# A norm's factor is moved from the hidden activations to the layer's outputs

## The chip, the cores and the metric

The kernel runs on one core of a Trainium2 chip. The metric is the device time of one execution in microseconds (us), the median of several runs. The core has five engines with queues of their own, each worked through in order: PE (TensorE, matmuls into PSUM), DVE (VectorE), ACT (ScalarE), POOL (GpSimd) and SP, which here only starts transfers. ACT starts some transfers too.

## The reference

One layer of a decoder on 1032 tokens (1024 of a prompt and 8 of a decode batch). Three head groups come first; the change lies behind them, in the output projection, the second norm and the feed-forward part:

```python
x = x + mix @ w_out                       # (1032, 1024)
h2 = rms_norm(x, norm2_g)                 # x * rsqrt(mean(x*x) + 1e-6) * g, per token
x = x + square(relu(h2 @ w_ff1)) @ w_ff2  # 1024 -> 4096 -> 1024
```

The factor of the norm is one positive number per token. Relu lets it through, the square squares it, and the second product is linear in it, so `1 / (mean(x*x) + 1e-6)` may multiply the squared activations or the 1024 outputs of the second product.

## The kernel before

Everything is kept with features on the 128 partitions and tokens along the columns. A tile of 1032 columns is cut in two halves of 516 (`TH`), and a half in two quarters of 258 (`TQ2`). The matmuls work on numbers that are split into a rounded part (hi) and a rest (lo): a `split` is a cast on ACT and a subtraction on DVE or POOL, and each product is three matmuls (hi·hi, hi·lo, lo·hi). In the profile a split of weights has the tile name `w`, one of activations `xy`, `xe`, `xf`, `xa` (first product) or `hf` (second).

`out_proj` makes x after the head groups in eight tiles, adds up their squares in the tile `r2` (shown as `r`), and at its end turns the sum into the factor: three matmuls with a tile of ones, and on DVE three scalings and three reciprocals of 344 columns each. `x_late` then makes the last forms of x that the first product needs.

Both feed-forward products use a scheme with seven block products in place of eight. The **first product** (`ffn_up`) runs over 16 items `j`. Each has seven products of 24 matmuls (168 in all), called 0 to 6 below. DVE adds the results out of PSUM (`t<-pq`), ACT applies relu and square to two tiles of 1032 columns, DVE multiplies each by `r2` (`t<-t,r`), makes four differences, and ACT's queue stores seven half tiles in DRAM (`hs`). PSUM has four buffers `pq`. The weights of an item come as four raw tiles (a11, a12, a21, a22), of which `w_forms` makes four sums s1 to s4 on POOL and seven splits; five of the splits are on POOL, two on DVE. Three more raw tiles per item go through `w_sums`, which makes sums for the second product (two on POOL). The seven raw tiles per item share six buffers (`wf` 2, `wf2` 4) in turn, so each load has to wait until the tile six places before it was read for the last time. The splits of weights have seven buffers (`w` 4, `w2` 3).

The **second product** (`ffn_down`) has seven groups in the order i = 5, 1, 6, 2, 7, 3, 4, each with four items o of 96 matmuls. Written (7,2) below is item o = 2 of group 7. In one item, the weights of the next are split (`w_tile`: four splits on POOL, in groups 7 and 3 each behind a subtraction of two raw tiles on DVE), the activations of the next group are loaded back and split on DVE (`hf`, two of 1032 columns per item, up to group 3), and the results are gathered in `p5`, `p1`, `u2` (shown as `acc`; `u3` is `u2`'s place, `u4` is `p1`'s). x itself comes back from DRAM by `x1` and is added on POOL, and `put` stores a half tile of the output from SP's queue. Results, loaded x and differences of weights share the six buffers `st` (`hx`).

The order on each queue is not the program's: a scheduler lays out all instructions before the run, by its own simulation, and the queues keep that order.

## Time and profile before

| | |
|---|---|
| median of 3 runs | 1522.04 us (1516.54 to 1531.46) |
| profiled execution | 1524.57 us, its span 1522.0 us |
| PE busy | 1384.9 us (91%) |
| DVE busy | 962.7 us (63%) |
| POOL busy | 824.2 us (54%) |
| ACT busy | 562.1 us (37%) |
| the first product on PE | 828.27 to 1185.31 us of the span |
| the second product on PE | 1185.31 us to the end |

The profile is one execution; all later stretches are microseconds from its start. PE is the busiest engine, but an average over 1522 us hides stages with different limits, so the stages have to be read one by one.

### The profile page before, as it was taken

The page shows a single profiled execution, that of the slowest core. Times are in us where ns is not written, and L with a number is a line of the kernel's source. Part 1 is how long each engine was busy: PE and PEld are TensorE (multiplying, and loading weights), DVE is VectorE, ACT ScalarE, POOL GpSimd, SP SyncE. Part 2 cuts the span into 40 slices and gives each one's busy share as a digit, 9 for nine tenths or more (in the row PEclk, how much of TensorE's full clock was granted, in tenths as well). Part 3 has the DMA queues.
Part 4 walks back from the last instruction along what each step waited for, and adds up shares of the span by engine and source line. Part 5 has one row for each costly group of instructions (what it writes and reads, how often), then busy time and mean ns, then how long its engine had stood idle before and what let it go on. Part 6 is the DMA issues. An engine that isn't in the chain of part 4 may idle for free.

```text
span 1522.0 us, 29392 instructions
## 1 busy us (share of the span) xinstructions
PE 1384.9 (91%) x11391; PEld 1276.8 (84%) x11391; DVE 962.7 (63%) x1656; ACT 562.1 (37%) x1057; POOL 824.2 (54%) x953
## 2 busy tenths in 40 slices
PE   5899799989889599797999699999999999999998
PEld 5888788879777477564898699999999999999998
DVE  7657457657666746775445987878778553328730
ACT  6433223233233243343444443444334454423430
POOL 7012673461144556350135887878778565678852
PEclk9899999899888667768899899999999999999999
DMA  6143233314433722234722265546655996469850
GB/s 236 61 162 111 86 89 101 94 58 122 118 114 95 187 66 54 79 100 128 287 84 98 76 216 202 194 172 212 215 209 195 356 319 199 148 220 306 286 171 35
DMA packets 152070, 238.17 MB, mean 156 GB/s; under 512 B 40851, under 2 KB 63340, under 8 KB 151788
## 3 DMA queue, kind: packets, MB, share of 16 engines
q1 hardware_dynamic: 132892, 191.77, 39.1%
q10 hardware_dynamic: 13824, 37.98, 6.4%
q0 software_dynamic: 5216, 6.56, 1.9%
q8 instruction: 89, 1.46, 0.4%
q14 instruction: 49, 0.40, 0.1%
HBM read 165.22 MB, written 72.08 MB: 156 GB/s over the span
## 4 chain that ended last, share of the span: by engine, by line
PE 43%; POOL 18%; DVE 12%; DMA 12%; issue 9%; ACT 3%; SPq 2%; POOLq 0%; DVEq 0%; ACTq 0%
PE pq L85 15%; PE d L85 14%; PE g L85 9%; POOL st L53 7%; POOL w L53 6%; POOL inv L53 5%; DMA wf<-in_w_ff 3%; PE cx L85 2%; DVE st L53 2%; SPq L82 2%; PE cy L85 2%; DMA qs<-xs 1%; PE g L89 1%; DMA x<-in_xT 1%; DVE F L53 1%
## 5 line engine op out<-in xcount | busy, mean ns | idle before, releaser
L85 PE MATMUL pq<-hf,w 128*128 128x258 f32 x2688 | 326.6, 284 | 6.1 <-ACT hf L76 2.8
L85 PEld LDWEIGHTS pq<-hf,w 128*128 128x128 f32 x2688 | 325.2, 190 | 7.4 <-ACT hf L76 3.0
L53 POOL TENSOR_TENSOR w<-wf,w 128x512 fp32r<-128x512 f32 x114 | 177.1, 1562 | 118.5 <-ACT w L76 118.4
L85 PE MATMUL d<-hbig,w 128*128 128x344 f32 (+2 forms) x1296 | 221.9, 327 | 19.3 <-ACT w L76 9.2
L85 PEld LDWEIGHTS d<-hbig,w 128*128 128x128 f32 x1296 | 202.3, 199 | 32.5 <-ACT w L76 10.4
L76 ACT CAST w<-wf 128x512 fp32r<-128x512 f32 x190 | 116.8, 618 | 217.2 <-PE pq L85 87.8
L53 POOL TENSOR_TENSOR w<-st,w 128x512 fp32r<-128x512 f32 x80 | 134.0, 1695 | 7.3 <-ACT w L76 7.3
L53 DVE TENSOR_TENSOR hf<-t,hf 128x1032 fp32r<-128x1032 f32 x56 | 97.2, 1776 | 54.6 <-ACT hf L76 54.6
L76 ACT CAST w<-st 128x512 fp32r<-128x512 f32 x96 | 58.9, 617 | 181.7 <-POOL st L53 78.6
L85 PE MATMUL pq<-xe,w 128*128 128x258 f32 x768 | 100.4, 291 | 10.6 <-POOL w L53 10.6
L85 PEld LDWEIGHTS pq<-xe,w 128*128 128x128 f32 x768 | 97.7, 197 | 11.6 <-POOL w L53 11.6
L53 DVE TENSOR_TENSOR t<-pq,t 128x516 f32<-128x516 f32 x112 | 75.9, 690 | 43.0 <-PE pq L85 41.0
L53 POOL TENSOR_TENSOR inv<-inv,blk 128x54 f32<-128x54 f32 (+24 forms) x217 | 71.3, 328 | 55.9 <-DMA out_state_p<-sl 20.3
L85 PE MATMUL pq<-xy,w 128*128 128x258 f32 x768 | 97.1, 286 | 1.6 <-DVE t L53 0.9
L85 PEld LDWEIGHTS pq<-xy,w 128*128 128x128 f32 x768 | 95.4, 193 | 2.7 <-ACT xy L76 1.7
L53 POOL TENSOR_TENSOR st<-wf,wf 128x512 f32<-128x512 f32 x48 | 69.9, 1455 | 40.0 <-DMA wf<-in_w_ff 27.7
L53 DVE TENSOR_TENSOR w<-wf,w 128x512 fp32r<-128x512 f32 x76 | 69.8, 919 | 29.2 <-ACT w L76 28.5
L53 POOL TENSOR_TENSOR inv<-inv,inv 128x54 f32<-128x54 f32 (+24 forms) x217 | 78.6, 362 | 15.9
L85 PE MATMUL pq<-xf,w 128*128 128x258 f32 x576 | 75.8, 288 | 11.6 <-DVE xf L53 8.3
L85 PEld LDWEIGHTS pq<-xf,w 128*128 128x128 f32 x576 | 72.8, 195 | 12.5 <-DVE xf L53 8.7
L53 DVE TENSOR_TENSOR t<-t,r 128x1032 f32<-128x1032 f32 x32 | 59.9, 1871 | 22.1 <-ACT t L73 22.0
L73 ACT ACTIVATE t<-t 128x1032 f32<-128x1032 f32 x64 | 68.1, 1064 | 14.5 <-DVE t L53 14.2
(405 smaller groups left out, 2620.1 us busy)
## 6 DMA issues: line engine op xcount, KB each, us to landing
wf<-in_w_ff SPq DMA_DIRECT2D x208, 256.0 KB
t<-hs SPq DMA_DIRECT2D x56, 516.0 KB
hs<-t ACTq DMA_DIRECT2D x48, 516.0 KB
wf<-in_w_in SPq DMA_DIRECT2D x34, 256.0 KB
tmp<-xs SPq DMA_DIRECT2D x32, 256.0 KB
wf<-s2s SPq DMA_DIRECT2D x32, 256.0 KB
x<-in_xT SPq DMA_DIRECT2D x8, 516.0 KB
xs<-xs SPq DMA_DIRECT2D x24, 172.0 KB
```

Of the source, the lines that this page charges most:

```text
L53: return (e or self.nc.vector).tensor_tensor(out, a, b, op=op)
L73: return self.nc.scalar.activation(out, a, f, **k)
L76: return self.nc.scalar.copy(out, a)
L82: return self.nc.sync.dma_start(out=out, in_=a)
L85: return self.nc.tensor.matmul(out, l, r, start=start, stop=stop, **k)
L89: return self.nc.tensor.transpose(out, a, ident)
```

## The change

The factor is no longer made at the end of `out_proj`. A new function `norm2` makes it after the eighth item of the first product, in two halves of 516 columns, with two of the PSUM buffers `pq`. The two multiplications per item of the squared activations are dropped. In the second product each output half tile is multiplied by the factor before x is added: twelve on DVE in `fin`, four on POOL (`u3`), four on DVE straight out of PSUM in the last group. The additions of x move behind the multiplications. Beside that, one split of weights per item of the first product, that of s3, goes from POOL to DVE.

```diff
@@ out_proj
-        for t0, tn in TG:
-            p = self.ps("g")
-            self.mm(p[:, :tn], self.ones, acc[:, t0:t0 + tn])
-            self.ts(acc[:, t0:t0 + tn], p[:, :tn], 1.0 / 1024, ALU.mult, 1e-6, ALU.add)
-            nc.vector.reciprocal(acc[:, t0:t0 + tn], acc[:, t0:t0 + tn])
@@ w_forms
         self.sub(s3, a11, a21, g)
-        r.append(self.w_form(s3, g))
+        r.append(self.w_form(s3, v))
@@
+    def norm2(self):
+        acc = self.r2
+        for h in range(2):
+            p = self.psp.tile([128, 2, 512], F32, name=self.nm("pq"), tag="pq", bufs=4)
+            for g in range(2):
+                self.mm(p[:, g, :TQ2], self.ones, acc[:, h * TH + g * TQ2:h * TH + g * TQ2 + TQ2])
+            sl = slice(h * TH, h * TH + TH)
+            self.ts(self.two(acc[:, sl]), p[:, :, :TQ2], 1.0 / 1024, ALU.mult, 1e-6, ALU.add)
+            self.nc.vector.reciprocal(acc[:, sl], acc[:, sl])
@@ ffn_up
                 self.act(h, h, AF.Relu)
                 self.act(h, h, AF.Square)
-                self.mul(h, h, self.r2)
@@
             up(j, ws)
             ws = nxt
+            if j == 7:
+                self.norm2()
@@ ffn_down
+            r2 = lambda t: self.r2[:, t * TH:t * TH + TH]
+
+            def fin(d, t, y):
+                self.mul(y, y, r2(t))
+                self.add(y, y, x1(d, t), g)
+                put(d, t, y)
@@
             elif i == 6:
                 plus(u2[:, o], p1[:, o])
-                self.add(p1[:, o], p1[:, o], x1(o, 0), g)
             elif i == 2:
                 y = self.hx()
                 plus(y, p1[:, o])
-                put(o, 0, y)
+                fin(o, 0, y)
                 self.add(u4[:, o], u2[:, o], p5[:, o], g)
-                self.add(p5[:, o], p5[:, o], x1(o + 4, 1), g)
-                self.add(u4[:, o], u4[:, o], x1(o, 1), g)
             elif i == 7:
                 plus(u3[:, o], u2[:, o])
                 y = self.hx()
                 self.add(y, u3[:, o], p5[:, o], g)
-                put(o + 4, 1, y)
+                fin(o + 4, 1, y)
+                self.mul(u3[:, o], u3[:, o], r2(0), g)
                 self.add(u3[:, o], u3[:, o], x1(o + 4, 0), g)
             elif i == 3:
                 y = self.hx()
                 plus(y, u4[:, o])
-                put(o, 1, y)
+                fin(o, 1, y)
             else:
                 y = self.hx()
-                plus(y, u3[:, o])
+                self.mul(two(y), p, two(r2(0)))
+                self.add(y, y, u3[:, o])
                 put(o + 4, 0, y)
```

Three places in the laid-out order follow. In these rows the numbers behind a name tell tiles apart.

**First place: POOL between two items of the first product, before.** `st` with two `wf` inputs or `st` and `wf` is a sum, `w` a split. The third row is s4, which reads raw tile a12 (`wf_9515`) for the last time; the row `w_9771` splits the next item's a11 (`wf_9763`), which is loaded into the same buffer.

```order
666 L53 TENSOR_TENSOR st_9537<-wf_1366_9513,wf_1368_9517 128x512
667 L53 TENSOR_TENSOR w_1375_9534<-st_9527,w_1375_9534 128x512
668 L53 TENSOR_TENSOR st_9542<-wf_9515,st_9528 128x512
669 L53 TENSOR_TENSOR w_9531<-st_9528,w_9531 128x512
670 L53 TENSOR_TENSOR w_1377_9539<-st_9537,w_1377_9539 128x512
671 L53 TENSOR_TENSOR w_9771<-wf_9763,w_9771 128x512
672 L53 TENSOR_TENSOR st_9757<-wf_1393_9753,wf_1394_9755 128x512
673 L53 TENSOR_TENSOR w_9774<-wf_1398_9765,w_9774 128x512
674 L53 TENSOR_TENSOR st_9758<-st_9757,wf_9751 128x512
675 L53 TENSOR_TENSOR st_9777<-wf_1399_9767,wf_9769 128x512
```

The same place on POOL after:

```order
662 L53 TENSOR_TENSOR st_9519<-wf_1363_9495,wf_1365_9499 128x512
663 L53 TENSOR_TENSOR w_1372_9516<-st_9509,w_1372_9516 128x512
664 L53 TENSOR_TENSOR st_9524<-wf_9497,st_9510 128x512
665 L53 TENSOR_TENSOR w_9513<-st_9510,w_9513 128x512
666 L53 TENSOR_TENSOR w_9751<-wf_9743,w_9751 128x512
667 L53 TENSOR_TENSOR st_9737<-wf_1390_9733,wf_1391_9735 128x512
668 L53 TENSOR_TENSOR w_9754<-wf_1395_9745,w_9754 128x512
669 L53 TENSOR_TENSOR st_9738<-st_9737,wf_9731 128x512
670 L53 TENSOR_TENSOR st_9757<-wf_1396_9747,wf_9749 128x512
```

The split of s3 (`w_1377_9539<-st_9537`) is gone, so one instruction instead of two stands between s4 and the split of the next a11.

**Second place: DVE at the end of the eighth item of the first product, before.** The tiles of this item are `t_1505` to `t_1507`; the first two rows are its last two results out of PSUM, `t_1537` is the next item's first.

```order
1332 L53 TENSOR_TENSOR t_1506_10551<-pq_10684,t_1506_10551 128x516
1333 L53 TENSOR_TENSOR t_1507_10552<-pq_10714,t_1507_10552 128x516
1334 L53 TENSOR_TENSOR t_1506_10551<-t_1506_10551,r_7742 128x1032
1335 L53 TENSOR_TENSOR w_10547<-wf_10519,w_10547 128x512
1336 L53 TENSOR_TENSOR t_1505_10550<-t_1506_10551 128x516
1337 L53 TENSOR_TENSOR w_1503_10544<-st_10542,w_1503_10544 128x512
1338 L53 TENSOR_TENSOR t_1507_10552<-t_1507_10552,r_7742 128x1032
1339 L53 TENSOR_TENSOR t_1537_10801<-pq_10829,t_1536_10800 128x516
1340 L53 TENSOR_TENSOR t_1505_10550<-t_1507_10552,t_1505_10550 128x516
```

The same place on DVE after; here the eighth item's tiles are `t_1502` to `t_1504`, and `t_1536` is the next item's:

```order
1320 L53 TENSOR_TENSOR t_1503_10525<-pq_10658,t_1503_10525 128x516
1321 L53 TENSOR_TENSOR w_1498_10513<-st_10511,w_1498_10513 128x512
1322 L53 TENSOR_TENSOR t_1504_10526<-pq_10687,t_1504_10526 128x516
1323 L53 TENSOR_TENSOR t_1502_10524<-t_1503_10525 128x516
1324 L67 TENSOR_SCALAR r_7742<-pq_10723 128x516
1325 L53 TENSOR_TENSOR w_10521<-wf_10493,w_10521 128x512
1326 L67 TENSOR_SCALAR r_7742<-pq_10728 128x516
1327 L53 TENSOR_TENSOR w_1500_10518<-st_10516,w_1500_10518 128x512
1328 L1364 RECIPROCAL r_7742<-r_7742 128x516 x2
1329 L53 TENSOR_TENSOR t_1502_10524<-t_1504_10526,t_1502_10524 128x516
1330 L53 TENSOR_TENSOR t_1503_10525<-t_1504_10526,t_1503_10525 128x516
1331 L53 TENSOR_TENSOR t_1536_10783<-pq_10811,t_1535_10782 128x516
```

The two multiplications by `r` are gone in every item; the split of s3 (`w_1498`) has come in, and in this one item the scalings and the two reciprocals stand ahead of the next item's first result.

**Third place: POOL during items (7,0) and (7,1) of the second product, before.** The first row is the output sum of (7,0), `st_15183` that of (7,1); `acc` with `st` is an addition of x, `w` a split of weights.

```order
881 L53 TENSOR_TENSOR st_15033<-acc_12740,acc_12738 128x516
882 L53 TENSOR_TENSOR w_14922<-st_14920,w_14922 128x512
883 L53 TENSOR_TENSOR w_15045<-st_15043,w_15045 128x512
884 L53 TENSOR_TENSOR w_2035_15054<-st_15052,w_2035_15054 128x512
885 L53 TENSOR_TENSOR acc_12740<-acc_12740,st_15036 128x516
886 L53 TENSOR_TENSOR w_2039_15063<-st_15061,w_2039_15063 128x512
887 L53 TENSOR_TENSOR st_15183<-acc_12740,acc_12738 128x516
```

The same place on POOL after, where the two output sums are `st_14979` and `st_15134`:

```order
857 L53 TENSOR_TENSOR st_14979<-acc_12706,acc_12704 128x516
858 L53 TENSOR_TENSOR w_14868<-st_14866,w_14868 128x512
859 L53 TENSOR_TENSOR acc_12706<-acc_12706,r_7742 128x516
860 L53 TENSOR_TENSOR w_14996<-st_14994,w_14996 128x512
861 L53 TENSOR_TENSOR w_2027_15005<-st_15003,w_2027_15005 128x512
862 L53 TENSOR_TENSOR st_14979<-st_14979,st_14982 128x516
863 L53 TENSOR_TENSOR acc_12706<-acc_12706,st_14987 128x516
864 L53 TENSOR_TENSOR w_2031_15014<-st_15012,w_2031_15014 128x512
865 L53 TENSOR_TENSOR st_15134<-acc_12706,acc_12704 128x516
```

From one output sum to the next there are eight instructions instead of six; the two new ones are the multiplication of u3 by `r` and the addition of x to the output, which waits for a multiplication on DVE.

## Rows read from the trace of the kernel before

**Rows 1.** Windows by stage: start:end, length, then per engine busy us (count), clock, DMA
```profile
822.00:828.27 6.27, 3.23 (x9) 1.34 (x8) 5.80 (x8) 4.07 (x6) 4.41 (x4) 0.79 0.62 208
828.27:863.83 35.56, 24.60 (x157) 23.69 (x157) 35.52 (x28) 12.22 (x21) 30.57 (x20) 0.75 0.16 53
863.83:1185.31 321.48, 309.39 (x2531) 308.09 (x2532) 254.25 (x230) 128.88 (x184) 256.48 (x166) 0.98 0.58 200
```
**Rows 2.** Timeline of PE in the first product: start, us, instruction, [idle before <-releaser]
```profile
887.14 5.93 PE L85 MATMUL pq<-xy,w 128*128 128x258 f32 x48
...
908.56 5.93 PE L85 MATMUL pq<-xy,w 128*128 128x258 f32 x48
...
928.66 5.93 PE L85 MATMUL pq<-xy,w 128*128 128x258 f32 x48
...
957.82 7.29 PE L85 MATMUL pq<-xe,w 128*128 128x258 f32 x46 [2.88 <-POOL w L53]
...
1021.79 5.80 PE L85 MATMUL pq<-xe,w 128*128 128x258 f32 x46 [1.84 <-POOL w L53]
```
**Rows 3.** Chain of waits, 960 to 1030: shares by engine and line
```profile
by line: POOL st L53 31.7%; POOL w L53 22.6%; issue 21.5%; DMA wf<-in_w_ff 12.8%; PE pq L85 11.9%; POOLq L53 0.2%
```
**Rows 4.** Whom POOL waited for, 880 to 1180: total us, times, longest
```profile
POOL st L53 <- DMA wf<-in_w_ff: 27.7, 7, 6.1
POOL w L53 <- ACT w L76: 24.4, 13, 2.9
```
**Rows 5.** Timeline of POOL, ACT and DVE within one item
```profile
1043.48 1.74 POOL L53 TENSOR_TENSOR w<-wf,w 128x512 fp32r<-128x512 f32 x1
...
1045.69 2.31 DVE L53 TENSOR_TENSOR t<-t,r 128x1032 f32<-128x1032 f32 x1
...
1048.46 0.62 ACT L76 CAST w<-wf 128x512 fp32r<-128x512 f32 x1 [5.20 <-DVE t L53]
...
1049.16 1.34 POOL L53 TENSOR_TENSOR w<-wf,w 128x512 fp32r<-128x512 f32 x1 [2.25 <-ACT w L76]
...
1050.97 3.42 DVE L53 TENSOR_TENSOR t<-pq,t 128x516 f32<-128x516 f32 x5
```
**Rows 6.** Groups by shape, 880 to 1160: busy us, mean ns
```profile
L53 POOL TENSOR_TENSOR w<-st,w 128x512 fp32r<-128x512 f32 x39 | 64.7, 1676 | 0.0
```
**Rows 7.** All instructions on the factor's tile: ns least/median/most
```profile
L53 DVE TENSOR_TENSOR t<-t,r x32: 1217/1850/2333, 868.0 to 1194.9; 128x1032 f32<-128x1032 f32 x32
L53 POOL TENSOR_TENSOR r<-r,st x14: 1292/1301/1491, 753.8 to 823.7; 128x516 f32<-128x516 f32 x14
...
L1221 DVE RECIPROCAL r<-r x3: 2290/2294/2295, 824.0 to 831.2; 128x344 f32<-128x344 f32 x3
```
**Rows 8.** Timeline of PE where the second product begins
```profile
1185.31 5.69 PE L85 MATMUL pq<-hf,w 128*128 128x258 f32 x46
1193.77 0.87 PE L85 MATMUL pq<-hf,w 128*128 128x258 f32 x4 [2.77 <-ACT hf L76]
```
**Rows 9.** Chain of waits at the same place: start, us, what
```profile
1181.68 5.81 DMA hs<-t
1187.57 5.08 DMA t<-hs
```
**Rows 10.** Groups by shape, 1374 to 1422 (items of group 7)
```profile
L53 POOL TENSOR_TENSOR w<-st,w 128x512 fp32r<-128x512 f32 x16 | 28.4, 1795 | 0.0
```
**Rows 11.** Windows: group 7, and a short one after a wait of PE
```profile
1374.00:1422.00 48.00, 47.07 (x392) 46.76 (x391) 37.40 (x30) 17.67 (x25) 41.82 (x25) 1.00 0.93 310
...
1436.00:1438.00 2.00, 1.97 (x11) 1.97 (x12) 0.21 (x1) 0.00 (x0) 2.00 (x2) 0.65 0.96 296
```
**Rows 12.** Timeline of PE in the second product
```profile
1396.10 37.39 PE L85 MATMUL pq<-hf,w 128*128 128x258 f32 x310 [0.93 <-POOL w L53]
...
1436.04 81.97 PE L85 MATMUL pq<-hf,w 128*128 128x258 f32 x670 [1.17 <-POOL w L53]
```
**Rows 13.** The last instruction of the timeline
```profile
1518.12 0.69 DVE L53 TENSOR_TENSOR st<-pq,acc 128x516 f32<-128x516 f32 x1 [10.79 <-PE pq L85]
```

## The prediction

> **What bounds the kernel now.** I read the stages first, as windows: the change touches what lies behind 822 us, and the first window to look at is the first product. Its granted clock is 0.98 and PE is busy for nearly all of it [rows 1], so it looks PE-bound. The timeline of PE shows that it isn't quite. An item that waits for nothing takes 928.66 - 908.56 = 20.10 us; the 14 items from 887.14 to 1185.31 took 298.2 us where 14 x 20.10 = 281.4 would do, so 16.8 us are lost, and each wait ends with a split of weights on POOL [rows 2, 8]. The waits come once in three items: from one to the next it is 1021.79 - 957.82 = 64.0 us for three items, against 60.3 at PE's rate [rows 2]. The chain of waits over such a turn runs through POOL, with PE at 11.9% of it [rows 3]. So POOL sets the pace, by a little. Why POOL needs 64 us is in the next two views. It is kept waiting by loads of raw weights and by casts on ACT [rows 4], and within an item one sees where the second comes from: DVE multiplies by the factor (2.31 us), ACT's cast comes late because its queue stands at the store of the multiplied tiles ("<-DVE t", 5.20 us), and POOL's split then waits 2.25 us for that cast [rows 5]. The second product is PE-bound but for three short waits: at its start, where PE waits for activations that come back from DRAM [rows 8, 9], and in groups 7 and 3, where it waits for splits of weights [rows 12].
>
> **The multiplications dropped and the split moved (first product).** I count POOL's turn of 64.0 us. Removed: three splits of s3 at 1.68 [rows 6], 5.0. Given back: a buffer that s4 frees is filled again for the next a11, and now one split instead of two passes meanwhile (first place of the order); that is so in two of three items, and POOL already waits about 4 us (27.7 in 7) where nothing hides a load [rows 4]. So 2 x 1.7 = 3.4 of the 5.0 come back as waiting. The waits for ACT's casts are 24.4 us in 300, about 5.1 per turn [rows 4]; DVE's differences and with them the stores come two multiplications (median 1.85 each [rows 7]) earlier, so I take 3.5 of them as gone. Contention: a POOL instruction of this size takes 1.30 alone [rows 7] and 1.74 beside DVE [rows 5], so every DVE instruction on two SBUF tiles costs POOL up to 0.44; two go and one comes per item, 1.4 per turn. Together 5.0 - 3.4 + 3.5 + 1.4 = 6.5, and 64.0 - 6.5 = 57.5 is under 60.3: PE sets the pace, and the whole **16.8 us** come back. The other end: all of the split returns as waiting and no wait for ACT goes; then the turn is 62.6, 2.3 over, and 14 items gain only 16.8 - 10.7 = 6.1. I take the upper end, since the turn has 2.8 us to spare in the middle estimate.
>
> **A wait that is added.** DVE's split of s3 waits for POOL and ACT, and results out of PSUM stand behind it on DVE (second place: `w_1498` ahead of `t_1504`). While POOL is ahead that costs nothing; for the few items in which it isn't I charge **2.0 us** (0 to 8).
>
> **norm2 in the eighth item.** PE's work is the same 1032 columns as before (3 x 344, now 4 x 258), but it now stands between two items that would otherwise follow at once. It was at most the 3.23 us of PE in its old window [rows 1]; I take 2.0. DVE gets two scalings out of PSUM, like an addition out of PSUM 3.42 / 5 = 0.68 [rows 5], and two reciprocals of 2.29 x 516 / 344 = 3.44 [rows 7]: 8.3 us. Queued behind them is the next item's first result, whose buffer PE needs again for product 5. PE reaches that after 2.0 + 5 x 20.10 / 7 = 16.4 us; DVE, with three splits or differences ahead and two behind the reciprocals at 1.2 to 1.7 each, after some 15 to 17.4 us. So 0.5 on the path, **2.5 us** in all (0 to 10.3, the upper end if all 8.3 of DVE is in the way).
>
> **What leaves the entry of the first product.** From 828.27 to 863.83 DVE is busy for 35.52 of 35.56 us, with PE waiting for x's last forms [rows 1]. Three reciprocals and three scalings leave DVE: 3 x 2.29 [rows 7] + 3 x 0.46 (0.68 cut to 344 columns) = 8.3 us, and two s3 splits of some 1.7 come, 3.4. That would be 4.9, but POOL is busy there for 30.57 us too [rows 1], and reciprocals, with one tile to read, hardly hold it up while the differences that move into their place do. I take **3.5 us** as gained (0 to 8.3).
>
> **The hand-over to the second product.** The first 50 matmuls would take 6.0 us and end at 1194.6 instead of 1191.3, with PE waiting 2.77 for a tile that was stored (5.81) and read back (5.08) [rows 8, 9]. The stores come two multiplications earlier, so nearly all of it goes: **3.0 us** gained (0 to 4).
>
> **The second product.** Per item of group 7 POOL has eight instructions instead of six (third place), eight more in the group, at 41.82 / 25 = 1.67 each over all kinds [rows 11] (its splits take 1.80 [rows 10]) 13.4 us. The four items take 4 x 96 / 168 x 20.10 = 46 us on PE, and POOL is idle for 48 - 41.8 = 6.2 us of its window [rows 11], so 7.2 are over. Group 2 loses four additions on POOL, but POOL can't run further ahead than the seven buffers of split weights; I give that 2.2. So PE waits **5.0 us** more, mostly at the beginning of group 3, where it waits already [rows 12]. The ends: 0, if the additions of x, which PE doesn't wait for, fall into gaps; 15, if nothing is hidden and the clock drops after each wait, as it did after 1436 (0.65 granted, between 1.2 and 2.4 GHz) [rows 11]. At the very end DVE has one more instruction before the last store, like the 0.69 of the last one [rows 13]: **0.7 us**.
>
> **The rule weighed.** A DVE instruction on two SBUF tiles slows a POOL instruction from 1.30 to 1.74 and is itself slowed, from 1.22 to 2.33 us for the multiplication, while the additions out of PSUM keep 0.68 [rows 5, 7]. The Trainium skill, "SBUF — State Buffer", section "Who interferes with whom", says that a VectorE instruction with two SBUF inputs and a GpSimd instruction that reads SBUF share one port and that the second one blocks fully. The rows agree in kind; the rule speaks against the change, which puts sixteen more such instructions on DVE and four more on POOL into groups that are already tight.
>
> **The sum.** 1524.57 - 16.8 + 2.0 + 2.5 - 3.5 - 3.0 + 5.0 + 0.7 = 1511.5 for the profiled execution, which stands 2.5 above the median of 1522.04. So **1509 us**, 0.9% less; its own range, half of the larger bounds, is 1503 to 1516.
>
> **Rivals.** *The second product hides its work.* For it: POOL's new instructions in group 7 are needed by nobody for 46 us; DVE was full at the entry, so all 8.3 may count there. Then 16.8 - 2.0 + 8.3 + 4.0 - 0.7 = 26.4 and the median is 1496. Against it: queues are in order, and the weights stand behind these instructions.
>
> *One port for two engines decides group 7.* If the two never work at once on SBUF, an item of group 7 costs its durations alone: eight of POOL at 1.30 and on DVE four differences and a multiplication at about 0.68 and two `hf` at 1.22 (the least for 1032 columns), 16.2 us against 11.5 on PE, four times 4.7; group 3 with five of POOL 12.3, four times 0.8. The same count for before gives 13.0, four times 1.5, so 16.3 us are lost in place of 5.0 and the median is 1520. Rows 11 and 12 speak against the full price, for they show less lost before than this count. It is what the rule of the page above would do here.
>
> *POOL's turn stays.* The moved split returns as waiting for loads, as at the other end above: 6.1 in place of 16.8, so 1520.
>
> *Slower: DVE and POOL wait for each other in turn.* In group 7 POOL's output sum waits for DVE's result, DVE's multiplication for that sum, and POOL's addition of x for the multiplication, with the differences and `hf` of coming items behind each on the two queues. If in groups 7 and 3 each of eight items so loses three POOL instructions of 1.7, 41 us go in place of 5.0: 1545. It is slower than before from some 18 us, 2.3 per item, on. Against it: the weights are split up to an item ahead.
>
> **How the numbers follow.** Chances: my sum 0.41, the second product hidden 0.27, the port 0.15, POOL's turn 0.10, the mutual waiting 0.07. A change of 1% (15.2 us) is about what a measurement here tells from none. Below 1506.8 lies some 0.3 of my case and nearly all of the second: 0.38. Above 1537.3 lies most of the last: 0.06. The rest is 0.56. The range reaches from the hidden case to just beyond the two cases at 1520: 1494 to 1526.
>
> **What would show it.** PE's items from the third on at 20.1 us without waits for POOL, except 2 to 3 us at the eighth; the entry a few us shorter; no wait at the hand-over; the waits around the start of group 3 longer. I am wrong if PE still waits for weights every third item, if DVE's split of s3 holds up results out of PSUM item after item, or if groups 7 and 3 cost PE more than 15 us.

## The result, and the profile after

The changed kernel takes 1508.9 us (median of 11 runs, 1502.49 to 1514.76), the kernel before 1525.42 us in the 11 runs beside it (1516.54 to 1531.46). The ratio is 0.9896, 95% interval 0.9875 to 0.9916, so the change makes the kernel 1.0% faster, just at the bound that the forecast drew between faster and no change. The profiled execution has a span of 1503.2 us, 18.8 less than before.

The program falls into four stretches, cut by the starts of PE's items in the timeline: up to the last matmul of out_proj (819.00, before 822.32), from there to item 2 of the first product, counted from 0 (the entry), from there to the second product, and the second product.

| stretch, us | before | after | difference | forecast |
|---|---|---|---|---|
| up to the end of out_proj (same code) | 822.3 | 819.0 | -3.3 | 0 |
| entry, to item 2 | 64.8 | 60.8 | -4.0 | -3.5 |
| first product, from item 2 | 298.2 | 283.3 | -14.9 | -12.3 |
| second product | 336.7 | 340.1 | +3.4 | +2.7 |

The first row is the scatter of unchanged code: over the kernels below, the end of out_proj lies between 816.5 and 831.1 us. What follows compares stretches behind it, which repeat far better: the changed kernel and the five below with its entry, but for at most one split, take 60.8 or 60.9 us there.

The windows of the changed kernel by stage (start:end, length, then busy us and count for PE, weight loads, DVE, ACT, POOL, the granted clock, DMA share, GB/s) answer to [rows 1]:

```profile
821.38:858.21 36.83, 26.79 (x157) 24.86 (x157) 33.95 (x28) 14.18 (x25) 34.18 (x22) 0.77 0.21 68
858.21:1163.13 304.92, 304.92 (x2540) 304.69 (x2541) 196.67 (x219) 134.62 (x188) 217.23 (x153) 1.00 0.63 221
```

The second line begins at item 1. From there on PE is busy for every microsecond of the first product, at a granted clock of 1.00 (before: 309.39 of 321.48 at 0.98). DVE is busy for 64% of it and POOL for 71%, where it was 79% and 80%. The timeline of PE, which answers to [rows 2], shows the same item by item:

```profile
899.97 5.93 PE L85 MATMUL pq<-xy,w 128*128 128x258 f32 x48
...
920.08 5.93 PE L85 MATMUL pq<-xy,w 128*128 128x258 f32 x48
...
1000.51 1.90 PE L85 MATMUL pq<-r,ones 128*128 128x258 f32 x8
1002.06 6.10 PE L85 MATMUL pq<-xy,w 128*128 128x258 f32 x48
...
1022.33 5.93 PE L85 MATMUL pq<-xy,w 128*128 128x258 f32 x48
```

No row of the first product from item 2 on has a bracket, so PE waits for nobody. An item takes 20.11 us; the eighth, from 980.40 to 1002.06, takes 21.7 with the eight matmuls on `ones` at its end. The chain of waits over 960 to 1030 went through POOL in [rows 3]; of the changed kernel it is one piece:

```profile
by line: PE pq L85 100.1%
```

POOL now waits for others, in the waits from 880 to 1160 (who waited for whom: us, times, longest), beside [rows 4], which reach to 1180:

```profile
POOL w L53 <- ACT w L76: 49.0, 19, 5.3
...
POOL st L53 <- DMA s2s<-st: 19.3, 4, 5.4
```

The 49.0 us are more than twice those of before (20.9 in the same window), and they are harmless, for PE waits for no split there. Of the 19 casts that POOL waited for, five had themselves waited for PE, and most others stood behind ACT's own relu and square. A longer wait of an engine that has stopped being the bound says nothing against it.

On DVE, the timeline around the factor (the scalings with splits of weights between and behind, the two reciprocals, two differences of activations, then results out of PSUM), with POOL's next pass below it:

```profile
1003.01 0.68 DVE L67 TENSOR_SCALAR r<-pq 128x516 f32<-128x516 f32 x1
1003.62 0.68 DVE L53 TENSOR_TENSOR w<-wf,w 128x512 fp32r<-128x512 f32 x1
1004.21 0.68 DVE L67 TENSOR_SCALAR r<-pq 128x516 f32<-128x516 f32 x1
1004.82 0.68 DVE L53 TENSOR_TENSOR w<-st,w 128x512 fp32r<-128x512 f32 x1
1005.42 6.60 DVE L1364 RECIPROCAL r<-r 128x516 f32<-128x516 f32 x2
1011.94 1.99 DVE L53 TENSOR_TENSOR t<-t,t 128x516 f32<-128x516 f32 x2
1013.86 1.28 DVE L53 TENSOR_TENSOR t<-pq,t 128x516 f32<-128x516 f32 x2
```

```profile
1006.01 1.30 POOL L53 TENSOR_TENSOR w<-wf,w 128x512 fp32r<-128x512 f32 x1 [3.48 <-ACT w L76]
```

The ninth item's results wait until 1013.86, 11.8 us behind its start, and PE doesn't notice.

The second product on PE, beside [rows 8, 12]:

```profile
1163.13 207.73 PE L85 MATMUL pq<-hf,w 128*128 128x258 f32 x1730
1371.12 12.03 PE L85 MATMUL pq<-hf,w 128*128 128x258 f32 x96 [0.26 <-POOL w L53]
...
1404.71 1.72 PE L85 MATMUL pq<-hf,w 128*128 128x258 f32 x12 [1.22 <-DVE hf L53]
...
1414.46 0.80 PE L85 MATMUL pq<-hf,w 128*128 128x258 f32 x2 [4.49 <-ACT w L76]
1416.62 81.93 PE L85 MATMUL pq<-hf,w 128*128 128x258 f32 x670 [1.35 <-POOL w L53]
```

The waits at the hand-over are gone. From (7,2), at 1371.12, to the start of (3,1), at 1414.46, PE waits in every item, for POOL, then for DVE's `hf`, and for 4.49 us for a cast whose difference DVE had made late, at 1412.00, behind five `hf` in a row. The granted clock is 0.50 from 1414 to 1416, which is the 1.2 GHz level, half of 2.4:

```profile
1414.00:1416.00 2.00, 0.80 (x2) 0.50 (x2) 2.00 (x2) 0.94 (x2) 2.00 (x2) 0.50 0.60 195
```

What DVE and POOL do meanwhile stands in their timelines, POOL first:

```profile
1364.21 1.76 POOL L53 TENSOR_TENSOR st<-acc,acc 128x516 f32<-128x516 f32 x1
1365.92 1.74 POOL L53 TENSOR_TENSOR w<-st,w 128x512 fp32r<-128x512 f32 x1
1367.63 1.75 POOL L53 TENSOR_TENSOR acc<-acc,r 128x516 f32<-128x516 f32 x1
...
1374.45 1.29 POOL L53 TENSOR_TENSOR acc<-acc,st 128x516 f32<-128x516 f32 x1
1375.70 1.29 POOL L53 TENSOR_TENSOR w<-st,w 128x512 fp32r<-128x512 f32 x1
1376.95 1.29 POOL L53 TENSOR_TENSOR st<-acc,acc 128x516 f32<-128x516 f32 x1
```

and DVE:

```profile
1364.73 1.78 DVE L53 TENSOR_TENSOR st<-wf,wf 128x512 f32<-128x512 f32 x1
1366.44 1.78 DVE L53 TENSOR_TENSOR st<-st,r 128x516 f32<-128x516 f32 x1
1368.14 1.79 DVE L53 TENSOR_TENSOR st<-wf,wf 128x512 f32<-128x512 f32 x1
...
1373.24 0.68 DVE L53 TENSOR_TENSOR acc<-pq,acc 128x516 f32<-128x516 f32 x1
1377.03 1.76 DVE L53 TENSOR_TENSOR st<-wf,wf 128x512 f32<-128x512 f32 x1 [3.10 <-POOL w L53]
...
1389.31 5.21 DVE L53 TENSOR_TENSOR st<-wf,wf 128x512 f32<-128x512 f32 x3 [3.08 <-DMA out_yT<-st]
...
1402.33 8.00 DVE L53 TENSOR_TENSOR hf<-t,hf 128x1032 fp32r<-128x1032 f32 x5
...
1412.00 3.44 DVE L53 TENSOR_TENSOR st<-wf,wf 128x512 f32<-128x512 f32 x2
```

Read the starts, not the durations. While both work, each starts a pass every 1.71 us, in step. While DVE is idle (1374 to 1377), POOL starts one every 1.25 us. DVE alone starts one every 0.60 us, as in the rows around the factor (1003.62 to 1004.82), where POOL stands idle for 3.48 us until 1006.01. 1.25 + 0.60 = 1.85, so a pair in 1.71 is hardly faster than one after the other. The two also wait for each other by data: in group 7 DVE stands idle twice, 3.10 us behind a split of POOL and 3.08 us behind the store of an output (1377.03 and 1389.31).

### The profile page after: what moved, and what is told of

Same layout as the page of the kernel before. It is cut to its first block, busy times and chain, and to the rows that moved or that the text cites. A ratio compares the mean times of both kernels' runs of the same rounds, so it can differ in the third digit from the quotient of the medians.

```text
span 1503.2 us, 29406 instructions
## 1 busy us (share of the span) xinstructions
PE 1376.0 (92%) x11393; PEld 1271.9 (85%) x11393; DVE 924.2 (61%) x1654; ACT 564.5 (38%) x1057; POOL 792.7 (53%) x941
## 4 chain that ended last, share of the span: by engine, by line
PE 65%; DVE 12%; POOL 8%; DMA 7%; issue 4%; ACT 3%; SPq 1%; POOLq 0%; ACTq 0%; DVEq 0%
PE pq L85 37%; PE d L85 14%; PE g L85 9%; POOL inv L53 4%; DVE st L53 2%; PE cx L85 2%; SPq L82 1%; PE g L89 1%; PE cy L85 1%; DMA qs<-xs 1%; DMA W<-ws 1%; DVE F L53 1%; DVE hf L53 1%; POOL w L53 1%; DMA ws<-inv 1%
## 5 line engine op out<-in xcount | busy, mean ns | idle before, releaser
L85 PE MATMUL pq<-hf,w 128*128 128x258 f32 x2688 | 326.6, 284 | 8.8 <-ACT w L76 4.5
L85 PE MATMUL d<-hbig,w 128*128 128x344 f32 (+2 forms) x1296 | 225.1, 330 | 19.8 <-ACT w L76 9.9
L85 PEld LDWEIGHTS d<-hbig,w 128*128 128x128 f32 x1296 | 205.4, 203 | 33.0 <-ACT w L76 11.1
L53 POOL TENSOR_TENSOR w<-st,w 128x512 fp32r<-128x512 f32 x64 | 99.9, 1569 | 6.9 <-ACT w L76 6.8
L85 PE MATMUL pq<-xe,w 128*128 128x258 f32 x768 | 95.1, 282 | 1.3 <-POOL w L53 1.3
L85 PEld LDWEIGHTS pq<-xe,w 128*128 128x128 f32 x768 | 93.1, 189 | 1.7 <-POOL w L53 1.7
L53 DVE TENSOR_TENSOR w<-wf,w 128x512 fp32r<-128x512 f32 x76 | 56.4, 742 | 33.0 <-ACT w L76 32.3
L85 PE MATMUL pq<-xa,w 128*128 128x258 f32 x576 | 73.1, 285 | 0.0
```

The costliest lines, as they stand in the source:

```text
L53: return (e or self.nc.vector).tensor_tensor(out, a, b, op=op)
L85: return self.nc.tensor.matmul(out, l, r, start=start, stop=stop, **k)
```

## The experiments

"Entry", "first" and "second" are the stretches of the table above in us, from each kernel's profiled execution; the time is a median, the ratio is to the kernel before, with its interval. Where an expectation says the second item of the first product, it is item 2.

**The split of s3 back on POOL.** The changed kernel with

```
-        r.append(self.w_form(s3, v))
+        r.append(self.w_form(s3, g))
```

> The changed kernel with the split of s3 back on POOL; all else as changed. Theory A (the multiplications were the cause: their time on DVE delayed ACT's casts and slowed POOL's passes): POOL's turn of three items is 64.0 - 3.5 (casts) - 2.6 (six passes on DVE fewer, 0.44 each) = 57.9 us, under PE's 60.3, so PE has no wait for POOL from the second item of the first product on, and the time is that of the changed kernel within 4 us, 0.990 to 0.993 of before, the rest at the entry, where three s3 splits return to POOL. Theory B (POOL's own instructions were the cause, and the moved split is what freed it): POOL's turn is 62 to 64 us, PE waits for weights in every third item again, 10 to 17 us are lost, and the ratio is 0.997 to 1.001.

Measured: 1511.48 us, ratio 0.9916 (0.9887 to 0.9946); entry 60.8, first 284.3, second 341.6. Theory A holds, B falls: PE waits for no split of POOL in the first product from item 2 on; the only wait is 0.78 us in that item, for DVE.

**The split of s3 alone.** The kernel before with

```
-        r.append(self.w_form(s3, g))
+        r.append(self.w_form(s3, v))
```

> The kernel before with one thing changed: the split of s3 goes to DVE, while the multiplications by the factor stay in the first product. Theory A (the multiplications were the cause): POOL's turn is 64.0 - 5.0 + 3.4 (waiting for loads) + 1.3 (one more pass on DVE per item) = 63.7 us, the waits of PE in every third item stay, and the ratio is 0.996 to 1.003, the more so since DVE gets a third long pass per item. Theory B (the moved split frees POOL): POOL's turn falls below 60.3 us, all 16.8 us come back, and the ratio is 0.987 to 0.991.

Measured: 1517.83 us, ratio 0.9949 (0.9926 to 0.9972); entry 63.3, first 294.0, second 336.3. Its timeline of PE keeps the waits, shorter:

```profile
952.67 3.75 PE L85 MATMUL pq<-xe,w 128*128 128x258 f32 x29 [0.97 <-POOL w L53]
...
1013.26 5.81 PE L85 MATMUL pq<-xe,w 128*128 128x258 f32 x46 [1.27 <-POOL w L53]
```

Neither range was met: the ratio lies between them. The waits stay, as A said, but 4.2 us of the 16.8 come back where its count gave (64.0 - 63.7) x 14 / 3 = 1.4. So moving a pass per item from POOL to DVE is worth something here, though about a quarter of what the multiplications are.

**The multiplications alone.** The kernel before, with the multiplication of the activations left out (nothing is scaled by the factor, which is still made):

```
                 self.act(h, h, AF.Square)
-                self.mul(h, h, self.r2)
```

> The kernel before without the two multiplications of the squared activations by the factor, which it leaves out (the factor is still made at its old place, nothing is multiplied by it); s3 stays on POOL, the second product is as before. Theory A (the multiplications were the whole cause in the first product, and most of the entry's gain too, since the first item's two stand there in DVE's full queue): from the end of out_proj to the second item 61 to 63 us instead of 64.8, from there to the second product 281.5 instead of 298.2, no wait at the hand-over, and the waits around the start of group 3 as before (6.5 us); together 20 to 24 us less, ratio 0.984 to 0.987. Theory B (it takes the moved split as well, or the factor's work must leave the entry): the entry stays at 64 to 65 us, or waits for POOL's splits stay in every third item, ratio 0.990 or more.

Measured: 1498.81 us, ratio 0.9814 (0.9771 to 0.9857); entry 63.5, first 283.1, second 330.3, together 22.8 less than before. PE's timeline from the second product on:

```profile
1165.12 204.87 PE L85 MATMUL pq<-hf,w 128*128 128x258 f32 x1706
1370.42 37.37 PE L85 MATMUL pq<-hf,w 128*128 128x258 f32 x310 [0.43 <-POOL w L53]
1409.24 0.51 PE L85 MATMUL pq<-hf,w 128*128 128x258 f32 x2 [1.45 <-ACT w L76]
1410.93 80.47 PE L85 MATMUL pq<-hf,w 128*128 128x258 f32 x670 [1.18 <-POOL w L53]
```

Theory A holds for the first product (15.1 of the 16.8 us) and for the hand-over, where no wait is left. At the entry it doesn't: 1.3 us were gained where 2 to 4 were expected. The ratio is a little under A's range.

**The factor at its old place.** The changed kernel with the loop over three column blocks back at the end of out_proj, and

```
             ws = nxt
-            if j == 7:
-                self.norm2()
```

> The changed kernel with the factor made at its old place, at the end of out_proj with three matmuls, while the outputs and not the activations are multiplied. Theory A (the gain at the entry of the first product, 4.0 us, comes from the factor's work leaving it): the stretch from the end of out_proj to the second item grows by 3 to 8 us, the eighth item gets its 1.7 us back, so the time is 1 to 6 us above the changed kernel, ratio to before 0.990 to 0.994. Theory B (the entry became shorter because the split of s3 left POOL, and the factor's work is hidden there): the entry stays, and the time is 1 to 2 us below the changed kernel, ratio 0.988 to 0.989.

Measured: 1509.09 us, ratio 0.9892 (0.9858 to 0.9926); entry 62.2, first 281.6, second 340.5. The entry grew by 1.4 us, less than A's 3 to 8 and not the nothing of B, and the eighth item got its 1.7 back. The time is that of the changed kernel. Making the factor in the eighth item is worth nothing.

**All output steps of group 7 put off.** The changed kernel with

```
             elif i == 7:
                 plus(u3[:, o], u2[:, o])
-                y = self.hx()
-                self.add(y, u3[:, o], p5[:, o], g)
-                fin(o + 4, 1, y)
-                self.mul(u3[:, o], u3[:, o], r2(0), g)
-                self.add(u3[:, o], u3[:, o], x1(o + 4, 0), g)
...
             else:
+                y = self.hx()
+                self.add(y, u3[:, o], p5[:, o], g)
+                fin(o + 4, 1, y)
+                self.mul(u3[:, o], u3[:, o], r2(0), g)
+                self.add(u3[:, o], u3[:, o], x1(o + 4, 0), g)
                 y = self.hx()
                 self.mul(two(y), p, two(r2(0)))
```

> The changed kernel with the output steps of group 7 (the sum u3 + p5, both multiplications by the factor, both additions of x, the store) put off to the items of group 4, where POOL has no weights left to split. Theory A (POOL's eight instructions per item are what makes PE wait in groups 7 and 3): with four per item POOL runs ahead, PE's waits between the start of group 7 and item (3,1), about 9 us with what the lower clock costs, go away, and the time is 6 to 10 us under the changed kernel, ratio to before 0.983 to 0.986. Theory B (the change of groups sets it, where DVE has to make the activations' eight hf splits and the next differences in a row, whatever POOL has to do): PE still waits 5 us or more at items (3,0) and (3,1), and the ratio is 0.988 to 0.990. A tail longer by 1 us or more would show that group 4 has no room for the steps.

Measured: 1493.4 us, ratio 0.9789 (0.9753 to 0.9825); second 327.0. It is the fastest version that computes everything. PE's whole second product is one row:

```profile
1166.46 322.27 PE L85 MATMUL pq<-hf,w 128*128 128x258 f32 x2688
```

So 340.07 - 327.04 = 13.0 us were lost in the changed kernel, more than the 6 to 10 expected: PE's waits there add up to 8.8 us, and the same 2688 matmuls take 326.6 us in place of 322.3, some of them at the lower granted clock that follows a wait (0.50 from 1414 to 1416). B's 5 us at (3,0) and (3,1) are not there. But this version takes away from POOL, from DVE and from the buffers at once; the next five take them apart.

**Only the steps on u3 put off.** As above, but y and `fin` stay in group 7.

> The changed kernel with only the multiplication and the addition of x on u3 put off from group 7 to group 4; the output sum, its multiplication on DVE, its addition of x and its store stay in group 7. POOL has six instructions per item there as in the kernel before, DVE has what it has after the change. Theory A (the number of POOL's instructions makes the waits): most of the 13 us that the second product loses against the version with all steps put off come back, down to the 6.5 of the kernel before or less; 6 to 13 us under the changed kernel, ratio 0.981 to 0.986. Theory B (DVE and the buffers decide: the output's tile is held until it is multiplied, added to and stored, DVE's next difference waits for such a buffer, and DVE comes late to the change of groups): the waits at (3,0) and (3,1) stay, and the time is within 3 us of the changed kernel.

Measured: 1504.67 us, ratio 0.985 (0.9819 to 0.9882); second 336.8. The edit did half of what it meant: in the laid-out order the multiplication of u3, which depends on nothing that comes later, still stands in group 7, and only the addition of x moved. So POOL has seven instructions per item, not six. The ratio lies in A's range, but the second product gained only 3.3 us, where A wanted 6 or more, for one POOL pass per item fewer.

**Only the steps on y put off.** The sum stays in group 7; the rest comes in group 4:

```
-                y = self.hx()
-                self.add(y, u3[:, o], p5[:, o], g)
-                fin(o + 4, 1, y)
+                self.add(p5[:, o], u3[:, o], p5[:, o], g)
...
             else:
+                y = self.hx()
+                self.mul(y, p5[:, o], r2(1))
+                self.add(y, y, x1(o + 4, 1), g)
+                put(o + 4, 1, y)
```

(The addition of x is on POOL; the expectation says DVE by mistake, which changes nothing in group 7.)

> The changed kernel with only the output steps of y put off from group 7 to group 4 (the sum u3 + p5 stays on POOL in group 7, written into p5; its multiplication by the factor, addition of x and store come in group 4, the addition on DVE). POOL has seven instructions per item of group 7 (eight after the change, six before), DVE no multiplication there, and no buffer waits for a store. Theory A (the number of POOL's instructions): of the 13 us only a part comes back, 2 to 6, and less than with the steps on u3 put off; ratio 0.986 to 0.989. Theory B (DVE and the buffers): nearly all 13 us come back, ratio 0.979 to 0.982.

Measured: 1504.57 us, ratio 0.9844 (0.9814 to 0.9873); second 331.0, 9.1 less than the changed kernel. PE's rows of it from the second product's start on:

```profile
1173.80 239.32 PE L85 MATMUL pq<-hf,w 128*128 128x258 f32 x1993
1413.91 1.70 PE L85 MATMUL pq<-hf,w 128*128 128x258 f32 x12 [0.79 <-DVE hf L53]
1416.15 13.25 PE L85 MATMUL pq<-hf,w 128*128 128x258 f32 x109 [0.53 <-DVE hf L53]
1430.95 69.06 PE L85 MATMUL pq<-hf,w 128*128 128x258 f32 x574 [1.55 <-POOL w L53]
```

In group 7 PE waits for nothing; the waits begin in group 3. By stretches theory A, which gave 2 to 6, falls: POOL has seven instructions as in the run before, and the second product is 5.8 us shorter. Theory B's "nearly all" of the 13 is not reached either. The ratios of the two can't be told apart, so this rests on the two traces alone.

From the runs up to here I had formed theory B of the next expectation: the loss goes with how many tiles of the ring `st` an item takes.

**One buffer more.** The changed kernel with

```
-        ... tag="st", bufs=6)[:, :n]
+        ... tag="st", bufs=7)[:, :n]
```

> The changed kernel with seven instead of six buffers of the ring st; the second product's instructions and their order on POOL are those of the changed kernel. From the runs so far, what is lost in the second product above the 327.0 us of the version with all steps put off goes with the tiles of st per item of group 7: 0 at four, 4.0 at five, 6.5 (before) and 9.7 at six, 13.0 at seven (changed). Theory B (the ring: differences of weights wait for a tile that is still held for an addition of x or a store): one buffer more is worth about as much as one tile per item less, 2 to 6 us, second product 334 to 338 us. Theory A (POOL's eight instructions per item): nothing changes there, 339 to 341 us.

Measured: 1518.32 us, ratio 0.9943 (0.992 to 0.9967); entry 60.2, first 289.2, second 341.7. Theory B falls: nothing came back in the second product. The kernel became slower elsewhere: with another buffer the order of DVE and ACT at the entry is laid out differently, and in item 2 PE waits for a split on DVE. In the trace that split stands on DVE's queue behind one that waited 2.37 us for a cast, ACT had waited for a sum on POOL, and POOL, at 881.69, 3.75 us for a load of raw weights; that the other order made this load late is likely, not shown.

```profile
893.49 1.23 PE L85 MATMUL pq<-xf,w 128*128 128x258 f32 x4 [3.10 <-DVE w L53]
...
905.95 5.95 PE L85 MATMUL pq<-xy,w 128*128 128x258 f32 x48
```

**One buffer more and one tile less.** As in the run before, and with the output of group 7 in p5:

```
-                y = self.hx()
-                self.add(y, u3[:, o], p5[:, o], g)
-                fin(o + 4, 1, y)
+                self.add(p5[:, o], u3[:, o], p5[:, o], g)
+                fin(o + 4, 1, p5[:, o])
```

> The changed kernel with seven buffers of st, and with the output of group 7 formed, multiplied and added to in p5 instead of in a tile of st. POOL keeps its eight instructions per item of group 7, DVE its multiplication; per item six tiles of st are taken, from seven buffers. Theory B (the ring): as with five tiles and six buffers, about 4 us are lost, second product 330 to 333 us. Theory A (POOL's eight instructions, DVE's multiplication): 338 to 341 us as in the changed kernel.

Measured: 1517.49 us, ratio 0.9931 (0.9905 to 0.9958); entry 60.3, first 290.8, second 342.2. The same verdict: the ring is not the cause, however well the points seemed to lie on a line.

**The multiplication of u3 on DVE.** The changed kernel with

```
-                self.mul(u3[:, o], u3[:, o], r2(0), g)
+                self.mul(u3[:, o], u3[:, o], r2(0))
```

> The changed kernel with the multiplication of u3 in group 7 on DVE instead of POOL: POOL has seven instructions per item, DVE one more; the ring st is used as in the changed kernel. Theory A (POOL's instructions): 1.67 us per item come back, up to 6.7 us, second product 333 to 336 us. Theory B (the ring and DVE): no gain, second product 339 us or more, since DVE comes later still to the differences and the hf splits. The rule that the two engines share one port gives the same time within 2 us, since the pass only changes its engine.

Measured: 1510.73 us, ratio 0.9891 (0.9861 to 0.992); second 339.1. Theory A (the number of POOL's instructions) falls too: a pass per item taken from POOL gained 1.0 us instead of up to 6.7. The pass only changed its engine, and the time stayed, as one shared port would have it. But theory B expected 339 us or more as well, by DVE coming late, and the trace shows that too: from 1355 to 1424 POOL now waits 6.5 us for casts of differences that DVE makes later, where the changed kernel has 1.3 us of it. So this run speaks against POOL's count alone and doesn't choose between the port and the late DVE. The wait at the start of (3,1) is there to the digit:

```profile
1422.38 0.80 PE L85 MATMUL pq<-hf,w 128*128 128x258 f32 x2 [4.49 <-ACT w L76]
1424.05 82.09 PE L85 MATMUL pq<-hf,w 128*128 128x258 f32 x670 [0.88 <-POOL w L53]
```

**Stores behind the casts.** The kernel before with the stores of an item's activations written behind the casts of a11 and a12 (`put_late`, called among the weights of item j + 1, issues the stores of item j - 1):

```
         r = [self.w_form(a11, g), self.w_form(a12, g)]
+        self.put_late()
         s1, s2 = sx(), sx()
```

> The kernel before with one thing changed: the stores of an item's activations are issued on ACT's queue behind the casts of a11 and a12 of the item after the next instead of ahead of them, so that these casts don't queue behind a store that waits for DVE's multiplications. Theory A1 (of what the multiplications cost POOL, the late casts are the part that decides): POOL's turn falls by 3.5 us to about 60.5, so the waits of PE in every third item nearly vanish and 13 to 17 us come back, ratio 0.989 to 0.992. Theory A2 (what decides is that POOL's passes run at 1.53 us beside the multiplications and at 1.39 without them, 36 passes in a turn, 5.1 us): the turn stays at 63 us or more, PE waits as before, ratio 0.997 to 1.003.

Measured: 1526.98 us, ratio 1.000 (0.9972 to 1.0027); first 301.7. The ratio is A2's, but the run decides nothing: in the order that is laid out from the new code the stores stand ahead of the casts again in places (at 1057.79 a cast of raw weights follows a store and waits 5.49 us for DVE), and ACT still waits 37.5 us for DVE's tiles between 900 and 1140, before 36.4.

**Two scalings for each multiplication.** The kernel before, with the factor left out of the activations:

```
-                self.mul(h, h, self.r2)
+                for _ in range(2):
+                    self.ts(h, h, 1.0, ALU.mult)
```

> The kernel before with each multiplication of the squared activations by the factor, which it leaves out, replaced by two scalings by 1.0 on DVE, in the same place of the queue and with the same waits, but with one tile to read instead of two. Theory A1 (what decides is where the passes stand, so that the stores and ACT's casts come late): PE's waits in every third item stay, first product from its second item 294 to 299 us, ratio 0.993 to 1.001. Theory A2 (what decides is that a pass with two tiles to read and POOL's passes lengthen each other): the waits go, 281.5 to 285 us there, ratio 0.981 to 0.988.

Measured: 1543.91 us, ratio 1.0085 (1.0055 to 1.0115); first 314.8, outside both ranges. The reason is in the durations, least/median/most in ns, of the scaling, and in the timelines of DVE and POOL at 1067:

```profile
L66 DVE TENSOR_SCALAR t<-t x64: 681/1657/1802, 876.8 to 1224.1; 128x1032 f32<-128x1032 f32 x64
...
1067.94 3.48 DVE L66 TENSOR_SCALAR t<-t 128x1032 f32<-128x1032 f32 x2
```

```profile
1067.42 1.74 POOL L53 TENSOR_TENSOR st<-wf,wf 128x512 f32<-128x512 f32 x1
```

A scaling of 1032 columns takes 0.68 us at the least, as at 876.76 where POOL stands idle, half of a multiplication's 1.22 [rows 7], and beside POOL 1.7 to 1.8 like other short passes; POOL's pass beside it takes 1.74. So one tile to read is no way out. The run didn't take the sharing away but doubled the number of passes, and beside POOL each cost DVE a turn of 1.7 us although it needs 0.68. It can't tell A1 from A2.

## Why the prediction was right

The forecast was 1509 us and a gain of 13.1 us in the profiled execution; measured were 1508.9 us and, behind out_proj, 15.5. That the time was met to 0.1 us is luck: the kernel before has a median of 1525.42 us beside the changed one, 3.4 above the one that the forecast starts from, and the gain was larger by about as much. By stretches the gain was 2.4 us larger than forecast, from errors that partly cancel (2.0 + 0.6 + 0.5 + 0.7 - 1.4). Point by point:

**POOL's pace in the first product.** All of the 16.8 us came back, as taken. That the multiplications did it is shown: without them PE lost next to nothing, with the split on POOL or on DVE, and the split alone gave 4.2. The count had said so without my drawing the conclusion, for 64.0 - 3.5 - 2.6 = 57.9 is already under 60.3 without the split. (The 1.4 per turn for contention in the prediction is 3 x 0.44 = 1.3; it changes nothing.) The term for contention was too small. POOL's mean pass between 880 and 1160 fell from 227.3 / 144 = 1.58 us to 203.5 / 140 = 1.45, and to 226.8 / 156 = 1.45 in the run that only leaves the multiplications out: 0.12 for each of the 33 passes in a turn, 4.1 us, where 0.44 for each multiplication gives 2.6. (The expectation that speaks of 36 passes counts one per item too many: 144 in 280 us are 33 in 64.) The 4.1 alone would bring the turn to 59.9, just under 60.3. How much late casts add to this stays open; the run that was to take them away didn't.

**The added wait of DVE** cost nothing where I charged 2.0: POOL was ahead all the time.

**norm2** cost 283.3 - 14 x 20.10 = 1.9 us against 2.5, all of it the matmuls.

**The entry** gained 4.0 against 3.5. From the run without multiplications (63.5) to the one that also moves the factor with s3 on POOL (60.8) it is 2.7; the other 1.3 are the multiplications of items 0 and 1, which I had not counted there, and on top of these the split of s3 made no difference; alone it gave 1.5 (64.8 to 63.3). With s3 on DVE, the factor is worth 62.2 - 60.8 = 1.4. So the factor's leaving is worth 1.4 to 2.7 at the entry and costs 1.9 in the eighth item.

**The hand-over** cost before (1195.04 - 1185.31) - 50 x 20.10 / 168 = 3.75 us, and costs nothing now; forecast 3.0.

**The second product.** The loss in groups 7 and 3 is 340.07 - 327.04 = 13.0 after and was 336.69 - 327.04 - 3.75 = 5.9 before, so the change costs 7.1, tail included, against 5.0 + 0.7. The sign and the place were right. The step that failed is the reason, "eight instructions instead of six" on POOL: taking one of them away from POOL and giving it to DVE changed next to nothing (1.0 us), and POOL with seven instructions loses 9.7 us or 4.0, according to what DVE has to do. Ordered by the passes of POOL and DVE's multiplications together per item of group 7, the second product takes:

| passes per item (POOL + DVE's multiplications) | second product |
|---|---|
| 4 + 0, all put off | 327.0 |
| 6 + 0, the kernel before without its multiplications | 330.3 |
| 6 + 0, less the wait at the hand-over: before, s3 alone, stores behind the casts, two scalings | 332.9, 331.7, 331.8, 333.6 |
| 7 + 0, steps on y put off | 331.0 |
| 7 + 1, addition on u3 put off | 336.8 |
| 7 + 2, multiplication of u3 on DVE | 339.1 |
| 8 + 1, changed kernel | 340.1 |
| 8 + 1, with s3 on POOL, with the factor at its old place | 341.6, 340.5 |
| 8 + 1, the two with seven buffers | 341.7, 342.2 |

That speaks for the rival of one port for two engines, in kind: the passes of both count as one queue. Its price was wrong, 16.3 us against 7.1; two likely reasons, not tested apart, are that POOL and DVE start group 7 with weights split ahead, and that a pair takes 1.71 us and not the 1.30 + 0.68 = 1.98 of its count. The lock-step of the two timelines is shown. That the sum decides is not shown: it rests on one move between engines, which a late DVE explains as well, and on the order of this table, whose versions differ in other groups too and spread by 3 us at the same count. All versions above 336 us in the table have one more thing in common that the others lack, DVE's multiplication between two passes of POOL on one tile of group 7. The changed kernel's waits don't decide it: DVE waits 3.1 us twice in group 7, and the longest wait of POOL, 5.3 us up to 1411.07, is for DVE's last result of group 7, which stands behind five `hf`.

The Trainium skill, "SBUF — State Buffer", section "Who interferes with whom", says that DVE and GpSimd have one pair of ports in common and that it goes to one of them for a whole instruction. By that rule a pair would take about the 1.25 + 0.60 = 1.85 us; it takes 1.71, 8% less. By the same section of the Trainium skill a `tensor_scalar` can take that pair too although it reads one tile, and the 0.68 us that became 1.66 agree.

The first product fits in part. In the run that only leaves the multiplications out, two passes per item left DVE, and POOL, which nobody had relieved, fell under PE's pace. But there the move of the split of s3 from POOL to DVE, which leaves the sum as it is, gave 4.2 us, so the sum is not all.

**The rest.** POOL's turn did not stay. The mutual waiting of the two engines, for which the prediction had 41 us, can't have cost more than the 13.0 us that all of group 7's steps cost. The case of a hidden second product is what the version with all steps put off reaches, by an edit and not by itself.

## What to carry to other kernels

Where VectorE and GpSimd both stream through SBUF, look at the passes of both before moving one: in this kernel moving a pass per item from POOL to DVE bought 1.0 us in group 7 and 4.2 in the first product, while removing two from DVE let POOL keep up there without a change of its own (15.1 us). When a step must move, look for the stage where these engines are idle: here the same steps cost 13 us in group 7 and nothing in group 4. And a line through a few measurements is a theory: the ring of buffers seemed to fit them and fell at the first run that touched it.

## What was not expected of the hardware

A short DVE pass on tiles in SBUF costs a whole turn beside POOL's: the scaling of 0.68 us and the difference of weights, 0.60 from start to start, both came to one start in 1.7 us. And one buffer more went with a first product that is 5.9 and 7.5 us longer, beside another order of instructions at its entry.
